# Score accumulators of one bank instead of two, and result stores behind the next unit's scores, in a fused encoder layer

## The chip, the cores and the metric

The kernel runs on one core of one Trainium2 chip. The metric is the device time of one execution in microseconds (us), the median of several runs. Before the change it is 2105.86 us (three runs, 2105.69 to 2107.47).

Engines are named as in the profile: PE (matmuls; PEld is its weight load), DVE (vector engine), ACT (scalar engine), POOL (GpSimd), SP (issues DMAs). ACT issues DMAs too; those rows have the name ACTq. PSUM is the memory that PE writes its sums to. It has eight banks; one bank holds 512 float32 numbers in each of 128 partitions.

## The reference

One layer of a bidirectional encoder over two sequences, one of 1024 tokens (prompt) and one of 512 (sample), 1024 features. Tokens lie on a grid 64 wide.

```python
xn = rmsnorm(x);  z = xn @ w_in     # -> qa, ka, va, qb, kb, vb, ga, gb
o_a = gqa_attention(rope(rmsnorm(qa)), rope(rmsnorm(ka)), va)      # branch A
# branch B: 8 heads of 64; each query sees a window of 8 x 16 tokens of the grid
s = einsum('bqhd,bkhd->bhqk', qi, kb) * scale + bias
s = where(mask, s, -1e30);  p = softmax(s);  o_b = einsum('bhqk,bkhd->bqhd', p, vb)
merged = sigmoid(ga) * (o_a @ w_proj_a) + sigmoid(gb) * (o_b @ w_proj_b)
x = x + merged @ w_out
x = x + square(relu(rmsnorm(x) @ w_mlp_up)) @ w_mlp_down
y = rmsnorm(x)
```

## The kernel before

The sample sequence is worked on first, then the prompt, each through the input projection, branch A, branch B, the gated merge and the output projection; the MLP of both follows. Float32 matmuls are made of three: each operand is split into a high and a low part (names ending in h and l), and L266, L267 and L268 multiply high by high, low by high and high by low parts. The splits are an ACT copy (L255) and a DVE subtraction (L261).

**Branch B** (phase phB, around 170 to 310 us for the sample and 765 to 1040 for the prompt) is cut into units. A unit is one head and one strip of 16 columns of the prompt's grid, 32 units in all, or one head and a pair of strips of the sample's, 16 units. A unit has two halves: two halves of the rows for the prompt, the two strips for the sample. In names such as sbs1_7_2 stand the sequence (0 sample, 1 prompt), the head and the strip; a last 0 or 1 is the half (for the sample, the strip).

*s_unit* makes the scores. For each half POOL adds bias and mask (bms, L1150), PE runs two matmuls (sbs, L1164) of 384 key columns (256 for the sample), DVE adds the bias, negates and keeps the minimum (sbss, and the read of its accumulator, msbs, both L1166), and ACT takes the Exp (pbs, L1170). Both halves of a unit write into one PSUM tile of two banks, each into its own bank.

*planes* (prompt only) scales and splits the probabilities (L1184 and L1185 on DVE, hbs on ACT L1191 and DVE L1192), and SP issues their DMA transposes into bhs (L1195). *t_unit* does the same job for the sample with PE transposes (L1209 to L1215).

*v_unit* multiplies by the values (obs, L1237), brings the sum out on ACT (ot_Bs, L1244) and DVE (os_Bs, L1245; L1250 for the sample), and lets POOL add its two parts (L1263). For heads 0 to 5, ACT then issues the store of os_Bs to DRAM (obds, L1265, 64 KB, 36 stores in all). For heads 6 and 7 the result stays on the chip: ACT copies it (oXs, L1275) and DVE subtracts (L1276). Two os_Bs tiles take turns.

The loop over units is a pipeline of three: in its turn i it calls planes(i-1), s_unit(i), t_unit(i-1) and v_unit(i-2). In between it pulls matmuls of other work into the gaps, so that PE has something to do while DVE, ACT and POOL are busy with a unit: the projections of the gates (gps), of the next heads' queries and keys (pqbs, pkbs), and near the end of the loop branch A's output projection (ppas), whose sums DVE multiplies by gates (mAs, L1047).

What the program says is not the order on the engines. A scheduler sorts the instructions of each engine by priority and by when it thinks that they can run; each engine then executes its list in order, and waits at an instruction until all that it depends on is done. Dependencies go by whole tiles: an instruction that writes to a tile of which another engine has yet to read a part waits for that read, whatever columns each of them touches.

**PSUM** is shared by two pools: pbig, two tiles of two banks, from which a unit's scores are taken, and pmm, four tiles of one bank for everything else in this phase.

Of the kernel before, what the change touches and what calls it, by code (L numbers as in the profile page):

```python
# [19 lines left out]
P = 128  # L20
D = 1024
NC8 = D // P
HD = 64
# [51 lines left out]
def encoder(ctx: ExitStack, tc: tile.TileContext, xs, outs, w):  # L75
# [11 lines left out]
    rawp = mix.enter_context(tc.tile_pool(name="rawp", bufs=3))  # L87
    sgp = mix.enter_context(tc.tile_pool(name="sgp", bufs=2))
    s8l = mix.enter_context(tc.tile_pool(name="s8l", bufs=NLEFT))
    pbig = mix.enter_context(tc.tile_pool(name="pbig", bufs=2, space=bass.MemoryType.PSUM))  # L90
    pmm = mix.enter_context(tc.tile_pool(name="pmm", bufs=4, space=bass.MemoryType.PSUM))


    hd = dram.tile([NTOK, D], F32, name="hd")
# [2 lines left out]
    def phase(name, bufs=2):  # L97
        return tc.tile_pool(name=name, bufs=bufs, reuse_waits="tile")
# [8 lines left out]
        return pmm.tile([P, 512], F32, tag="mm", name=name)  # L107

    def big(name):
        return pbig.tile([P, 1024], F32, tag="big", name=name)  # L110


    ident = cst.tile([P, P], F32, name="ident")
# [379 lines left out]
    def run(tr, nxt, first):  # L493
# [560 lines left out]
        nkc = kr_n // 4  # L1054
        nkey = kr_n * 32
        nq = rows * 16
        with phase(f"phB{N}") as ph:
            JN = 3 - halves
            msk = ph.tile([P, halves * 3, nkey], BF16, tag="msk", name=f"msk{N}", bufs=1)
# [71 lines left out]
            qk = {}  # L1131
            W = halves * P

            def s_unit(u):
                h, js = u
                s = big(f"sb{N}_{h}_{js[0]}")
                p = ph.tile([P, 2, nkey], F32, tag="pb", name=f"pb{N}_{h}_{js[0]}", bufs=2)
                nm_, l, rl = (
                    sml.tile([P, 8], F32, tag=n_, name=f"{n_}b{N}_{h}_{js[0]}") for n_ in ("ms", "ss", "rs")
                )  # L1140
                for x, (j, hf) in enumerate((j, hf) for j in js for hf in range(halves)):
                    nm = f"{N}_{h}_{j}_{hf}"
                    ct = (0, 1, 1, 2)[j]
                    c0 = (0, 8, 24, 32)[j]
                    jr = (16, 8, 8, 0)[j]
                    r0 = 0 if hf == 0 else 4
                    ir = 4 if hf == 0 else 0
                    if j != 2:
                        bm = ph.tile([P, nkey], F32, tag="bm", name=f"bm{nm}", bufs=4)
                        nc.gpsimd.tensor_tensor(  # L1150
                            bm.rearrange("p (r c) -> p r c", c=32),
                            rects[h][:, ir : ir + kr_n, jr : jr + 32],
                            msk[:, hf * 3 + ct, :].rearrange("p (r c) -> p r c", c=32),
                            op=ALU.add,
                        )
                        bms[hf] = bm
                    bm = bms[hf]
                    q0 = j * (T // 4) + hf * P
                    so = s[:, x * 512 : x * 512 + nkey]
                    for i in range(2):  # L1160
                        kv = qk[h // 2][1][h % 2][:, i, :].rearrange("p (r c) -> p r c", c=GRID_W)[
                            :, r0 : r0 + kr_n, c0 : c0 + 32
                        ]
                        nc.tensor.matmul(so, qk[h // 2][0][:, h % 2, q0 : q0 + P], kv, start=(i == 0), stop=(i == 1))  # L1164
                    sb = ph.tile([P, nkey], F32, tag="sb", name=f"sbs{nm}", bufs=2)
                    nc.vector.tensor_tensor_reduce(  # L1166
                        out=sb, in0=so, in1=bm, op0=ALU.add, op1=ALU.min, scale=-1.0, scalar=3e38,
                        accum_out=nm_[:, x : x + 1],
                    )
                    nc.scalar.activation(  # L1170
                        p[:, x], sb, AF.Exp, bias=nm_[:, x : x + 1], scale=-1.0, accum_out=l[:, x : x + 1]
                    )
                    if JN == 2:
                        nc.vector.reciprocal(rl[:, x : x + 1], l[:, x : x + 1])
                        nc.gpsimd.tensor_scalar(p[:, x], p[:, x], rl[:, x : x + 1], 1.0, op0=ALU.mult, op1=ALU.mult)
                PT[u] = p
                if JN == 1:
                    rls[u] = l, rl
# [39 lines left out]
            def v_unit(u):  # L1218
                h, js = u
                nm = f"{N}_{h}_{js[0]}"  # L1220
                hl = PT.pop(u)
                o = mm(f"ob{nm}")
                if halves == 2:
                    ov = o.rearrange("p (i h q) -> p i h q", i=2, h=2)
                    seq = [
                        (ov[:, :, a:b, :], kc, js[0], hl[:, kc, :, a:b, :], n == 0, n == 3)
                        for n, (kc, a, b) in enumerate([(1, 0, 2), (2, 0, 2), (0, 0, 1), (3, 1, 2)])
                    ]
                else:
                    ov = o.rearrange("p (x i q) -> p x i q", x=2, i=2)  # L1230
                    seq = [
                        (ov[:, x], kc, j, hl[:, 2 * x + kc, :, 0, :], kc == 0, kc == 1)
                        for x, j in enumerate(js)
                        for kc in range(2)
                    ]
                for dst, kc, j, part, first_, last_ in seq:
                    nc.tensor.matmul(  # L1237
                        dst, strips[h][:, j, kc, :], part, start=first_, stop=last_, skip_group_check=True
                    )
                ps = slice(64 * (h % 2), 64 * (h % 2) + 64) if h >= 6 else slice(0, 64)  # L1240
                t = ph.tile([HD, 512], F32, tag="ot", name=f"ot_B{nm}", bufs=1)
                b = ph.tile([P, 512], F32, tag="os", name=f"os_B{nm}", bufs=2)[ps]
                if JN == 1:
                    nc.scalar.activation(t, o[HD:P], AF.Copy, scale=svs[HD:P, 6 + h // 4 : 7 + h // 4])  # L1244
                    nc.vector.scalar_tensor_tensor(  # L1245
                        b, o[0:HD], svs[0:HD, 6 + h // 4 : 7 + h // 4], t, op0=ALU.mult, op1=ALU.add
                    )
                else:
                    nc.scalar.activation(t, o[HD:P], AF.Copy)
                    nc.vector.tensor_tensor(b, o[0:HD], t, op=ALU.add)  # L1250
                if halves == 2:
                    b0, b1 = b[:, 0:256], b[:, 256:512]
                    def place(t_):
                        return t_[:, js[0] * 256 : js[0] * 256 + 256]

                else:
                    bv = b.rearrange("p (x i q) -> p x i q", x=2, i=2)
                    b0, b1 = bv[:, :, 0, :], bv[:, :, 1, :]
                    def place(t_):
                        v = t_.rearrange("p (j q) -> p j q", q=P)  # L1260
                        return v[:, 1:3] if js[0] == 1 else v[:, 0:4:3]

                nc.gpsimd.tensor_tensor(b0, b0, b1, op=ALU.add)  # L1263
                if h < 6:
                    nc.scalar.dma_start(place(obd[h * HD : h * HD + HD, :]), b0)  # L1265
                    return
                if not oX3:
                    oX3.append(slot([P, 2, T], F32R, f"oX{N}_1_3"))
                def token(t_):
                    v = t_.rearrange("p (r j c) -> p j r c", j=4, c=16)  # L1270
                    return v[:, js[0]] if halves == 2 else v[:, 1:3] if js[0] == 1 else v[:, 0:4:3]

                hi, lo = (token(oX3[0][ps, i, :]) for i in range(2))
                b0 = b0.rearrange("p (r c) -> p r c" if halves == 2 else "p x (r c) -> p x r c", c=16)
                nc.scalar.activation(hi, b0, AF.Copy)  # L1275
                nc.vector.tensor_tensor(lo, b0, hi.bitcast(F32), op=ALU.subtract)  # L1276

            prep(0)
            fill.add(gate(3328, zg[1]))
# [11 lines left out]
            for i in range(n + LS + LV):  # L1291
# [5 lines left out]
                    planes(units[i - 1])  # L1297
                if i < n:
                    s_unit(units[i])
                    if units[i][1][0] == 1 and units[i][0] + 1 < 8:  # L1300
                        prep(units[i][0] + 1)
                    if i % per == (6 if JN == 1 else 2) and i + 2 < n:
                        while held:
                            held.pop(0)()
                        qp = qkproj(i // per + 1, wqk, qk)
                        for _ in range(NC8):
                            next(qp)
                    if i % per == per - 1 and qp is not None:
                        for _ in qp:
                            pass  # L1310
                        qp = None
# [15 lines left out]
                        next(qp)  # L1327
                fill.pull(f - f // 2)
                if 0 <= i - LS - LV < n:
                    v_unit(units[i - LS - LV])  # L1330
            fill.drain()


        mgs = {}
        with phase(f"phG{N}") as ph:
            oX = load_o(1) + oX3
# [792 lines left out]
```

## Time and profile before

| | before |
|---|---|
| median of the runs | 2105.86 us (2105.69 to 2107.47) |
| the profiled execution | 2107.32 us |
| its span, from first to last instruction | 2105.5 us |
| PE busy | 2071.3 us, 98% of the span |
| DVE busy | 1500.9 us, 71% |
| ACT busy | 1137.8 us, 54% |
| POOL busy | 330.4 us, 16% |
| mean granted PE clock | 0.997 |

The profile is of one execution. In a row of a timeline stand the start, the time taken, the engine, the line, the operation, out<-in with tile names without their numbers, shapes, and, in square brackets, how long the engine had been idle before it and what ended that. Matmuls overlap, so the rate of PE is read from the starts of successive ones and not from the time that one takes. In a list of waits stand the waiting instruction, what it waited for, the sum in us, how often, and the longest.

### The profile page before, as it was taken

To read this page: it belongs to the slowest core of one execution; us is meant where nothing else is said; L and a number is where in the kernel's file an instruction comes from. 1 tells how busy PE (TensorE), PEld (TensorE's weight loads), DVE (VectorE), ACT (ScalarE), POOL (GpSimd) and SP (SyncE) were. 2 spreads that over 40 slices of the span, in tenths; PEclk is the share of its full clock that TensorE was granted. 3 is DMA by queue.
4 is the path that set the end of the run, shared out by engine and by line. 5 is a ranking of instruction groups with operands and counts; after the bars stand their busy time and mean duration, and the time that the engine had idled before them with its cause. 6 is when DMAs were issued, how large, how long until landed. Compare 5 with 4: busy or idle time off the path is not lost.

```text
span 2105.5 us, 31206 instructions
## 1 busy us (share of the span) xinstructions
PE 2071.3 (98%) x10521; PEld 1783.3 (85%) x10521; DVE 1500.9 (71%) x2885; ACT 1137.8 (54%) x2351; POOL 330.4 (16%) x445
## 2 busy tenths in 40 slices
PE   9999999999999999999999999999999999999998
PEld 8888878987797777777788999999999988888887
DVE  6775786778668855667864877787777777669563
ACT  5654654657647755666522666565556634334442
POOL 3232420422232222322101100012000000000000
PEclk9999999999999999999999999999999999999999
DMA  6546557645525565666764566478444899688561
GB/s 188 154 126 181 150 181 246 190 104 101 125 58 131 113 139 126 149 148 157 210 204 140 185 200 197 157 244 222 143 157 153 286 348 342 213 279 277 159 204 66
DMA packets 442569, 376.59 MB, mean 179 GB/s; under 512 B 167456, under 2 KB 380072, under 8 KB 442409
## 3 DMA queue, kind: packets, MB, share of 16 engines
q1 hardware_dynamic: 400471, 306.67, 50.4%
q10 hardware_dynamic: 36258, 50.88, 7.1%
q0 software_dynamic: 5680, 17.04, 2.9%
q8 instruction: 83, 1.36, 0.3%
q14 instruction: 77, 0.63, 0.1%
HBM read 263.29 MB, written 85.79 MB: 166 GB/s over the span
## 4 chain that ended last, share of the span: by engine, by line
PE 52%; DVE 1%; issue 1%; DMA 1%; ACT 1%; SPq 0%; POOL 0%; ACTq 0%; POOLq 0%; DVEq 0%
PE dn L267 7%; PE dn L268 7%; PE dn L266 7%; PE uc L266 2%; PE ud L266 2%; PE uc L268 2%; PE ud L268 2%; PE ud L267 2%; PE uc L267 2%; PE ua L266 2%; PE ua L268 2%; PE ua L267 2%; PE ops L267 1%; PE ops L268 1%; PE ops L266 1%; PE ub L266 1%
## 5 line engine op out<-in xcount | busy, mean ns | idle before, releaser
L268 PE MATMUL dn<-wd,al 128*128 128x512 f32 (+1 forms) x624 | 242.7, 389 | 0.0
L267 PE MATMUL dn<-wd,ah 128*128 128x512 f32 (+1 forms) x624 | 242.7, 389 | 0.0
L266 PE MATMUL dn<-wd,ah 128*128 128x512 f32 (+1 forms) x624 | 242.6, 389 | 0.0
L1542 ACT ACTIVATE ah<-ar 128x512 fp32r<-128x512 f32 x168 | 104.4, 627 | 202.5 <-PE dn L267 184.7
L1543 DVE TENSOR_TENSOR al<-ar,ah 128x512 fp32r<-128x512 f32 x168 | 115.0, 692 | 76.1 <-ACT ah L1542 68.1
L266 PEld LDWEIGHTS dn<-wd,ah 128*128 128x128 f32 x624 | 117.2, 188 | 24.2
L268 PEld LDWEIGHTS dn<-wd,al 128*128 128x128 f32 x624 | 117.2, 188 | 24.0
L267 PEld LDWEIGHTS dn<-wd,ah 128*128 128x128 f32 x624 | 117.2, 188 | 24.0
L903 ACT ACTIVATE ps<-ss,nms 128x1024 f32<-128x1024 f32 (+1 forms) x96 | 93.2, 971 | 33.9 <-DVE ls L911 11.9
L900 DVE TENSOR_REDUCE nms<-ss 128x1 f32<-128x1024 f32 (+1 forms) x96 | 99.7, 1039 | 13.9 <-PE ss L898 13.1
L266 PE MATMUL gpss<-xs_0h,w_gs 128*128 128x512 f32 x256 | 102.7, 401 | 1.4 <-DVE ptls L938 1.3
L267 PE MATMUL gpss<-xs_0l,w_gs 128*128 128x512 f32 x256 | 101.0, 395 | 0.0
L268 PE MATMUL gpss<-xs_0h,w_gs 128*128 128x512 f32 x256 | 100.7, 393 | 0.0
L251 POOL TENSOR_TENSOR rs_f<-ms_f,mhalf 128x1 f32<-128x1 f32 x6 | 4.0, 668 | 590.7 <-DVE ms_f L247 590.7
L1542 ACT ACTIVATE A<-S 128x512 fp32r<-128x512 f32 x128 | 76.1, 624 | 30.7 <-DVE S L1605 26.2
L1150 POOL TENSOR_TENSOR bms<-rects,msks 128x384 f32<-128x384 f32 (+1 forms) x72 | 64.2, 896 | 154.6 <-DVE msbs L1166 114.5
L1661 ACT ACTIVATE c<-c 128x384 f32<-128x384 f32 x97 | 50.7, 524 | 67.7 <-DVE c L1660 67.7
L1543 DVE TENSOR_TENSOR A<-S,A 128x512 fp32r<-128x512 f32 x128 | 84.5, 686 | 3.8 <-ACT A L1542 3.8
L1170 ACT ACTIVATE pbs<-sbss,msbs 128x384 f32<-128x384 f32 (+1 forms) x96 | 55.3, 577 | 58.8 <-POOL os_Bs L1263 23.3
L266 PE MATMUL uc<-B,A 128*128 128x384 f32 x256 | 85.7, 335 | 0.0
L266 PE MATMUL ud<-B,A 128*128 128x384 f32 x256 | 85.7, 335 | 0.0
L268 PE MATMUL uc<-B,A 128*128 128x384 f32 x256 | 85.7, 335 | 0.0
(391 smaller groups left out, 6369.2 us busy)
## 6 DMA issues: line engine op xcount, KB each, us to landing
ar<-ud SPq DMA_DIRECT2D x120, 512.0 KB
br<-in_w_mlp_down_dram SPq DMA_DIRECT2D x72, 512.0 KB
rawu<-in_w_mlp_up_dram SPq DMA_DIRECT2D x64, 512.0 KB
ud<-c ACTq DMA_DIRECT2D x128, 192.0 KB
raw_gs<-in_w_in_dram SPq DMA_DIRECT2D x32, 512.0 KB
zgs<-sgs ACTq DMA_DIRECT2D x48, 256.0 KB
ud<-cs SPq DMA_DIRECT2D x64, 192.0 KB
vss<-vds SPq DMA_DIRECT2D x256, 32.0 KB
```

Source lines behind the costliest of these rows:

```text
L251: nc.gpsimd.tensor_tensor(r[:, :n], m[:, :n], mhalf[:, :n], op=ALU.pow)
L266: nc.tensor.matmul(out, ah, bh, start=start, stop=False, **kw)
L267: nc.tensor.matmul(out, ah, bl, start=False, stop=False, **kw)
L268: nc.tensor.matmul(out, al, bh, start=False, stop=stop, **kw)
L900: nc.vector.tensor_reduce(nm_, s, axis=AX.X, op=ALU.max, negate=True)
L903: nc.scalar.activation(p, s, AF.Exp, bias=nm_, accum_out=l)
L1150: nc.gpsimd.tensor_tensor(bm.rearrange("p (r c) -> p r c", c=32), rects[h][:, ir : ir + kr_n, jr : jr + 32], msk[:, hf * 3 + ct, :].rearra ...
L1170: nc.scalar.activation(p[:, x], sb, AF.Exp, bias=nm_[:, x : x + 1], scale=-1.0, accum_out=l[:, x : x + 1])
L1542: nc.scalar.activation(hi, src, AF.Copy)
L1543: nc.vector.tensor_tensor(lo, src, hi.bitcast(F32), op=ALU.subtract)
L1661: nc.scalar.activation(t, t, AF.Relu)
```

## The change

1. In phase phB the score tiles come from a pool of four tiles of one bank, instead of two tiles of two banks. Each half of a unit takes its own tile. The pool is opened ahead of the phase and the one of two-bank tiles is opened again behind it. The pool pmm is now allocated ahead of it.
2. What follows POOL's addition in v_unit (the store for heads 0 to 5, the copy and the subtraction for heads 6 and 7) is put on a list and issued behind the s_unit of the loop's next turn, or, past the last s_unit, ahead of the next v_unit and at the end.

```diff
-    pbig = mix.enter_context(tc.tile_pool(name="pbig", bufs=2, space=bass.MemoryType.PSUM))
     pmm = mix.enter_context(tc.tile_pool(name="pmm", bufs=4, space=bass.MemoryType.PSUM))
+    bigs = mix.enter_context(ExitStack())
+    pbig = {}
+
+    def set_bigs(n):
+        bigs.close()
+        pbig.clear()
+        pbig[n] = bigs.enter_context(tc.tile_pool(name=f"pbig{n}", bufs=4 // n, space=bass.MemoryType.PSUM))
+
+    set_bigs(2)
...
-        return pbig.tile([P, 1024], F32, tag="big", name=name)
+        return pbig[2].tile([P, 1024], F32, tag="big", name=name)
...
+        set_bigs(1)
         with phase(f"phB{N}") as ph:
...
+            late = []
+
+            def put():
+                while late:
+                    late.pop(0)()
+
             def s_unit(u):
                 h, js = u
-                s = big(f"sb{N}_{h}_{js[0]}")
...
-                    so = s[:, x * 512 : x * 512 + nkey]
+                    so = pbig[1].tile([P, 512], F32, tag="one", name=f"sb{nm}")[:, 0:nkey]
...
                 nc.gpsimd.tensor_tensor(b0, b0, b1, op=ALU.add)
                 if h < 6:
-                    nc.scalar.dma_start(place(obd[h * HD : h * HD + HD, :]), b0)
+                    late.append(lambda: nc.scalar.dma_start(place(obd[h * HD : h * HD + HD, :]), b0))
                     return
...
-                nc.scalar.activation(hi, b0, AF.Copy)
-                nc.vector.tensor_tensor(lo, b0, hi.bitcast(F32), op=ALU.subtract)
+
+                def cut():
+                    nc.scalar.activation(hi, b0, AF.Copy)
+                    nc.vector.tensor_tensor(lo, b0, hi.bitcast(F32), op=ALU.subtract)
+
+                late.append(cut)
...
                     s_unit(units[i])
+                    put()
...
                 if 0 <= i - LS - LV < n:
+                    if i >= n:
+                        put()
                     v_unit(units[i - LS - LV])
+            put()
             fill.drain()
 
 
+        set_bigs(2)
```

In the changed file lines of this phase stand further down: L1164 becomes L1178, L1166 L1180, L1170 L1184, L1237 L1251, L1265 L1279, and L266 L274.

The scheduler's order moves with it in phase phB only. On PE, at the scores of unit 1_1_1, before:

```order
L1237 MATMUL obs1_0_2_9154<-bhs1_0_2_9039,vss1_0_8746 128x2x128
L1164 MATMUL sbs1_1_1_9176<-kBs1_0_1_8783,qBs1_0_8781 128x384 x2
L266 MATMUL gpss1_3328_1_0_9091<-xs1_0h1_4287,w_gs1_3328_1_8960 128x512
L267 MATMUL gpss1_3328_1_0_9091<-xs1_0l1_4289,w_gs1_3328_1_8960 128x512
...
L1164 MATMUL sbs1_1_1_9176<-kBs1_0_1_8783,qBs1_0_8781 128x384 x2
```

and with the change:

```order
L1251 MATMUL obs1_0_2_9186<-bhs1_0_2_9069,vss1_0_8774 128x2x128
L1178 MATMUL sbs1_1_1_0_9213<-kBs1_0_1_8811,qBs1_0_8809 128x384 x2
L1178 MATMUL sbs1_1_1_1_9221<-kBs1_0_1_8811,qBs1_0_8809 128x384 x2
L274 MATMUL gpss1_3328_1_0_9122<-xs1_0h1_4311,w_gs1_3328_1_8989 128x512
L275 MATMUL gpss1_3328_1_0_9122<-xs1_0l1_4313,w_gs1_3328_1_8989 128x512
```

The second half's pair stood four gate matmuls behind the first half's and now follows it directly. So it is with 47 of the 48 units; the one other is 1_7_2, of which the first half has moved into the next place.

On PE, where the scores of heads 6 and 7 begin, before:

```order
L268 MATMUL ppas1_0_1_11044<-oXs1_0_3_10913,w_pas1_0_10889 128x512
L1164 MATMUL sbs1_6_0_11100<-kBs1_3_0_10699,qBs1_3_10698 128x384 x2
L1164 MATMUL sbs1_6_3_11178<-kBs1_3_0_10699,qBs1_3_10698 128x384 x2
L1164 MATMUL sbs1_6_0_11100<-kBs1_3_0_10699,qBs1_3_10698 128x384 x2
L1164 MATMUL sbs1_7_1_11255<-kBs1_3_1_10700,qBs1_3_10698 128x384 x2
L1164 MATMUL sbs1_6_3_11178<-kBs1_3_0_10699,qBs1_3_10698 128x384 x2
L266 MATMUL ppas1_1_0_11066<-oXs1_0_0_10895,w_pas1_1_10985 128x512
```

and with the change:

```order
L276 MATMUL ppas1_0_1_11098<-oXs1_0_3_10965,w_pas1_0_10941 128x512
L1178 MATMUL sbs1_6_0_0_11159<-kBs1_3_0_10750,qBs1_3_10749 128x384 x2
L1178 MATMUL sbs1_6_0_1_11167<-kBs1_3_0_10750,qBs1_3_10749 128x384 x2
L1178 MATMUL sbs1_6_3_0_11237<-kBs1_3_0_10750,qBs1_3_10749 128x384 x2
L1178 MATMUL sbs1_6_3_1_11245<-kBs1_3_0_10750,qBs1_3_10749 128x384 x2
L1178 MATMUL sbs1_7_1_0_11315<-kBs1_3_1_10751,qBs1_3_10749 128x384 x2
L1178 MATMUL sbs1_7_1_1_11323<-kBs1_3_1_10751,qBs1_3_10749 128x384 x2
L1178 MATMUL sbs1_7_2_0_11382<-kBs1_3_1_10751,qBs1_3_10749 128x384 x2
L274 MATMUL ppas1_1_0_11120<-oXs1_0_0_10947,w_pas1_1_11038 128x512
```

Five pairs in a row have become seven; the second half of 7_1 and the first half of 7_2 have come forward. The second half of 7_2 stays about a hundred instructions behind, where both halves of it stood before.

On ACT, at the store of unit 1_0_3, before:

```order
L1244 ACTIVATE ot_Bs1_0_3_9303<-obs1_0_3_9298,svs_95 64x512
L1170 ACTIVATE pbs1_1_0_9321,ssbs1_1_0_9323<-sbss1_1_0_0_9329,msbs1_1_0_9322 128x384
L1265 DMA obds1_4442<-os_Bs1_0_3_9304 64x256
L1170 ACTIVATE pbs1_1_0_9321,ssbs1_1_0_9323<-sbss1_1_0_1_9336,msbs1_1_0_9322 128x384
L1191 ACTIVATE hbs1_1_2_1_9316<-pbs1_1_2_9259,rsbs1_1_2_9262 128x3x128
```

and with the change:

```order
L1258 ACTIVATE ot_Bs1_0_3_9337<-obs1_0_3_9332,svs_95 64x512
L1184 ACTIVATE pbs1_1_0_9353,ssbs1_1_0_9355<-sbss1_1_0_0_9362,msbs1_1_0_9354 128x384
L1184 ACTIVATE pbs1_1_0_9353,ssbs1_1_0_9355<-sbss1_1_0_1_9370,msbs1_1_0_9354 128x384
L1205 ACTIVATE hbs1_1_2_1_9349<-pbs1_1_2_9290,rsbs1_1_2_9293 128x3x128
L1279 DMA obds1_4466<-os_Bs1_0_3_9338 64x256
```

The store has moved from between the two Exps of the next scores to behind them and one more instruction. About a third of the stores move like this one; the others keep their places among the Exps.

## The prediction

> **What bounds the kernel now.** I read the page first, then PE's waits by stretch, then the busy windows of those stretches, then single moments on the timelines. The page says which engine sets the time.
>
> ```profile
> span 2105.5 us, 31206 instructions
> PE 2071.3 (98%) x10521; PEld 1783.3 (85%) x10521; DVE 1500.9 (71%) x2885; ACT 1137.8 (54%) x2351; POOL 330.4 (16%) x445
> ```
>
> PE is idle for 2105.5 - 2071.3 = 34.2 us in all. A change of this kind can win that idle time where it lies in branch B, whatever PE loses there to a lower clock, and what a matmul takes too long to start; nothing else. So the question is what PE waits for in branch B: about 170 to 310 us for the sample sequence, 765 to 1040 for the prompt. The waits of PE, for the three stretches 170 to 310, 765 to 960 and 960 to 1040, in this order:
>
> ```profile
> PE sbs L1164 <- DVE msbs L1166: 0.8, 3, 0.4
> PE ppas L266 <- ACT sgs L528: 0.7, 1, 0.7
> PE sbs L1164 <- DVE msbs L1166: 6.1, 11, 1.5
> PE sbs L1164 <- DVE msbs L1166: 6.6, 4, 3.8
> ```
>
> Columns are us in total, times, longest. One wait owns nearly all of it, 13.5 us in 18 pieces: a score matmul waits until DVE has read an accumulator. It is nearly always the second half of a unit, and what it waits for is the read of the first half, because both halves are one tile of two banks. The windows of the same stretches (length, busy time of PE, PEld, DVE, ACT, POOL, granted clock, DMA):
>
> ```profile
> 170.00:310.00 140.00, 138.00 (x680) 111.79 (x679) 94.81 (x247) 79.62 (x163) 49.96 (x72) 1.00 0.55 167
> 765.00:960.00 195.00, 188.57 (x848) 145.24 (x847) 126.03 (x314) 117.88 (x230) 52.90 (x57) 1.00 0.59 137
> 960.00:1040.00 80.00, 73.37 (x320) 55.64 (x319) 65.59 (x145) 45.01 (x90) 16.71 (x19) 0.96 0.77 185
> ```
>
> The first two have DVE at 68% and 65%, so DVE has room to follow an earlier PE. In the third it is at 82%, and the clock is not full.
>
> **The change part by part.** The order shows what moves: the second half's pair of matmuls, which stood two to six fill matmuls behind the first, now stands right behind it, on its own bank, and waits only for the read of four tiles back.
>
> *Scattered waits.* 0.8 + 6.1, and of the third stretch what its three long ones (1.52, 0.86 and 3.77, below) leave of 6.6, some 0.45: 7.3 us. With four banks PE may be two units ahead of DVE before it is held. I take 7.0; the bounds are 7.3, and 3 if half of them come back at the next instruction that needs DVE.
>
> *The longest wait.* PE, then DVE around it:
>
> ```profile
> 999.93 0.60 PE L1164 MATMUL sbs<-kBs,qBs 128*128 128x384 f32 x2
> 1001.08 0.40 PE L266 MATMUL ppas<-oXs,w_pas 128*128 128x512 f32 x1
> 1005.25 0.73 PE L1164 MATMUL sbs<-kBs,qBs 128*128 128x384 f32 x2 [3.77 <-DVE msbs L1166]
> 1005.77 0.63 PE L267 MATMUL ppas<-oXs,w_pas 128*128 128x512 f32 x1
> 1008.75 0.53 PE L268 MATMUL ppas<-oXs,w_pas 128*128 128x512 f32 x1
> 1009.12 0.39 PE L266 MATMUL ppas<-oXs,w_pas 128*128 128x512 f32 x1
> ```
>
> ```profile
> 998.09 0.76 DVE L261 TENSOR_TENSOR w_pbs<-raw_pbs,w_pbs 128x256 fp32r<-128x256 f32 x2 [2.30 <-ACT w_pbs L255]
> 1004.63 0.55 DVE L1166 CUSTOM_DVE_ANT_0 sbss<-sbs,bms 128x384 f32<-128x384 f32 x1
> 1005.11 0.08 DVE L1166 DVE_READ_ACCUMULATOR2_ANT msbs<- 128x1 f32 x1
> ```
>
> DVE had lost 2.30 us to a weight that was still in flight and then worked through its queue up to the scores of 7_2, while PE had work ready behind. After the change the second half of 7_2 waits for the bank of 6_3's second half, read long before. So 3.8 us go; 1.9 is the bound below, if half of DVE's lateness meets PE at its next use.
>
> *The clump.* Near 974 us five pairs of score matmuls stand in a row before, seven after, on four banks, so the fifth to seventh still wait:
>
> ```profile
> 974.33 0.87 PE L1164 MATMUL sbs<-kBs,qBs 128*128 128x384 f32 x4
> 976.72 0.62 PE L1164 MATMUL sbs<-kBs,qBs 128*128 128x384 f32 x2 [1.52 <-DVE msbs L1166]
> 978.21 1.52 PE L1164 MATMUL sbs<-kBs,qBs 128*128 128x384 f32 x4 [0.86 <-DVE msbs L1166]
> ```
>
> ```profile
> 971.42 0.56 DVE L1166 CUSTOM_DVE_ANT_0 sbss<-sbs,bms 128x384 f32<-128x384 f32 x1 [1.00 <-PE sbs L1164]
> 974.00 2.19 DVE L1192 SCALAR_TENSOR_TENSOR hbs<-pbs,rsbs,hbs 128x384 f16<-128x384 f32 x2
> 976.12 0.54 DVE L1166 CUSTOM_DVE_ANT_0 sbss<-sbs,bms 128x384 f32<-128x384 f32 x1
> 976.59 0.08 DVE L1166 DVE_READ_ACCUMULATOR2_ANT msbs<- 128x1 f32 x1
> ```
>
> The seventh pair needs three score reads and one hbs done on DVE: 3 x 0.55 + 0.1 + 2.19 / 2 = 2.9 us from the start of the first read. That start was 1.8 us behind the clump's (974.33 to 976.12); DVE's idle 1.00 at 971.42 goes and PE comes some 0.45 earlier, so I put it at 1.2. The seventh pair then starts 4.1 us after the clump's start. Unhindered it would start after six pairs: four matmuls took 0.87 to the end of the last, which with 0.34 for that last one is 0.177 from start to start, so 2.1 us. A wait of 2.0 stays of 2.38: gain 0.4, bounds -0.6 (DVE comes as late as before, 1.8) and 2.4.
>
> *The clock.* Both long stops are followed by slow matmuls. The windows of 10 us show it (the clock is the third number from the end):
>
> ```profile
> 970.00:980.00 10.00, 7.62 (x34) 5.68 (x32) 7.92 (x22) 6.78 (x16) 6.04 (x7) 0.92 0.47 106
> 980.00:990.00 10.00, 10.00 (x44) 7.36 (x43) 9.42 (x22) 5.24 (x11) 2.27 (x3) 0.91 1.07 237
> 1000.00:1010.00 10.00, 6.23 (x22) 4.89 (x21) 8.46 (x19) 5.98 (x13) 3.21 (x4) 0.83 0.57 157
> ```
>
> Behind the wait of 3.77, eight matmuls took from 1005.77 to 1009.12, 3.35 us; at the 0.23 apart of 1009.12 onwards they take 1.84. One drop costs 1.5. I take the second away and leave the clump's: 1.5, bounds 0 and 3.0. [...]
>
> *Opening a pair.* Where no wait shows, a pair still starts slowly:
>
> ```profile
> 818.11 0.60 PE L1164 MATMUL sbs<-kBs,qBs 128*128 128x384 f32 x2
> 818.55 0.40 PE L266 MATMUL pqbs<-xs_1h,w_bqs 128*128 128x512 f32 x1
> 819.48 0.62 PE L1164 MATMUL sbs<-kBs,qBs 128*128 128x384 f32 x2
> 819.94 0.40 PE L267 MATMUL pqbs<-xs_1l,w_bqs 128*128 128x512 f32 x1
> ```
>
> The pair holds PE for 0.44 (818.11 to 818.55), the second half's for 0.46, against 2 x 0.177 = 0.354 in the clump's first row: about 0.09 for each pair that stands alone. 47 of the 48 second halves now follow their first half directly: 47 x 0.09 = 4.2. I take 3.5; bounds 0 (the cost belongs to the bank, not to standing alone) and 4.6.
>
> *Stores and cuts.* The deferral hardly changes ACT's order: in about a third of the 36 stores it moves the store from between a unit's two Exps to behind them. What it touches:
>
> ```profile
> ACT pbs L1170 <- POOL os_Bs L1263: 23.3, 16, 2.7
> L1265 ACTq DMA_DIRECT2D obds<-os_Bs x36: 452/453/641, 204.8 to 986.9; - x36
> L1275 ACT ACTIVATE oXs<-os_Bs x12: 400/416/420, 295.1 to 1036.0; 64x256 fp32r<-64x256 f32 x12
> DVE os_Bs L1245: 0.4, 1
> ```
>
> The first row is ACT held at a store until POOL has added, and so the second Exp too; the last is DVE held once by a store in flight (from the list of who waited for the store). Behind the store on ACT stand the next Exp and hbs, and for these DVE waits. ACT is busy 118 of 195 us and PE waits for none of it, so I cost the step at nothing: the cover is the two units between a unit's scores and its v_unit. On POOL a few bias adds change places with their neighbours; on SP the transposes of hbs and some 32 KB loads of vss pass each other by a row or two, and the two queues gain no transfer. Without the cover, each of the prompt's eight deferred cuts brings the last projection 0.42 us later: bounds -3.4 and, for Exps that no longer stand behind a store, +1.
>
> *What comes back.* In the last stretch DVE would have to do its 65.6 us in about 80 - 6.6 = 73, 90%. I give back 1.2; bounds 5 and 0.
>
> Sum: 7.0 + 3.8 + 0.4 + 1.5 + 3.5 - 1.2 = 15.0. The profiled execution took 2107.3, so 2092.3; it lies 1.5 above the median of 2105.9, so in terms of that median 2090.8, say **2091**.
>
> **The rivals.**
>
> *Everything comes off.* DVE keeps up, the clump is smooth and the clock full: 7.3 + 3.8 + 2.4 + 3.0 + 4.6 = 21.1, which is 2084.7. For it: DVE idles in the clump for PE (1.00 at 971.42). Against: seven pairs on four banks.
>
> *The wait moves to DVE's next customer.* If DVE sets the pace of 960 to 1040, the 6.6 us return as waits of evacuated accumulators or of transposed planes, the clock drops stay, and half of the rest is kept: (0.8 + 6.1 + 4.2) / 2 = 5.5, so 2100.4. For it: the third window's 82%. Against: DVE lost 2.30 there to a transfer, not to work.
>
> [...]
>
> *It does not do what it says.* If these waits were for DVE's rate and not for the shared tile, the same time is lost elsewhere: about 2105.
>
> *Slower: the stores hold DVE.* There are two os_Bs buffers. A store that is issued later frees its buffer later, and DVE's L1245, which stands ahead of the next score reads, waits for it, as it did for 0.4 us. It decides from where the 24 stores of the prompt each hold DVE, and PE behind it, for (15.0 + 4.2) / 24 = 0.8 us; at 0.85 each the kernel is at 2105.9 - 15.0 + 20.4 = 2111. Against: a store moves by one Exp at most, and only in a third of the cases.
>
> **How the numbers follow.** The forecast has 0.47, everything 0.20, DVE's next customer 0.19, the clock 0.03, nothing 0.07, slower 0.04. A measurement here can tell about 0.2%, 4.2 us, from no change. So faster 0.89, the same 0.07, slower 0.04. The range goes from 2084, which takes in the full gain, to 2102, which takes in the moved wait.
>
> **What would show it.** Right: PE's wait for msbs falls from 13.5 to about 2, all of it near 974; no wait near 1005 and a granted clock of 1.00 there; second halves of 0.36 instead of 0.46 from start to start; the stretch from 765 to 1040 shorter by about 13. Wrong: new rows of PE waiting for mAs, os_Bs, bhs or sgs in the last stretch; more slow matmuls; DVE waiting for obds; or a clump that keeps both its waits and the later 3.8.

## The result and the profile after

The changed kernel takes 2089.48 us (median of four runs, 2087.87 to 2092.17) beside 2106.34 for the one before: a ratio of 0.9921, with a 95% interval of 0.9903 to 0.9938. The forecast was 2091, 2084 to 2102. The page of the profiled execution (2090.06 us):

```profile
span 2088.3 us, 31204 instructions
PE 2062.2 (99%) x10521; PEld 1782.6 (85%) x10521; DVE 1495.9 (72%) x2885; ACT 1137.3 (54%) x2351; POOL 330.1 (16%) x445
```

PE is busy 9.1 us less and idle 26.1 us instead of 34.2. The work is the same; it is busy for less time because pairs open without delay, one stretch of half clock is gone (1000 to 1010 at a granted clock of 0.83 before and 1.00 now), and a matmul overlaps with its successor where it used to run out ahead of a stop (ahead of the stop of 3.77 us one held PE from 1001.08 to 1001.48, 0.40 us, where 0.23 lie between the starts of others). PE's waits in the sample's branch B (170 to 310 us), and in the prompt's (765 to 953, and 953 to 1030):

```profile
PE ptbs L1223 <- POOL pbs L1189: 0.6, 2, 0.4
PE ppas L274 <- ACT w_pas L263: 0.6, 1, 0.6
PE ppas L274 <- ACT sgs L536: 0.3, 1, 0.3
...
PE obs L1251 <- DMA bhs<-hbs: 1.8, 2, 1.3
PE sbs L1178 <- DVE kBs L1136: 0.4, 1, 0.4
PE obs L1251 <- DVE hbs L1206: 0.3, 1, 0.3
...
PE sbs L1178 <- DVE msbs L1180: 2.1, 2, 1.7
PE obs L1251 <- DVE os_Bs L1259: 0.7, 1, 0.7
PE ppas L274 <- ACT w_pas L263: 0.3, 1, 0.3
```

The waits for msbs fell from 13.5 us to 2.1, and those 2.1 are the clump. New ones have come, of other kinds: PE now waits where the scores' work is used (obs, for the transposed planes and for os_Bs), and here and there for a weight. The windows (length, busy PE, PEld, DVE, ACT, POOL, granted clock, DMA):

```profile
170.00:310.00 140.00, 138.25 (x690) 114.21 (x689) 95.11 (x252) 80.53 (x164) 49.23 (x72) 1.00 0.56 169
765.00:950.00 185.00, 182.97 (x845) 146.48 (x845) 126.94 (x314) 118.38 (x233) 54.42 (x57) 1.00 0.62 142
950.00:1027.00 77.00, 73.16 (x323) 54.90 (x322) 62.68 (x143) 44.08 (x88) 15.94 (x19) 0.98 0.81 198
960.00:970.00 10.00, 7.74 (x28) 5.15 (x28) 8.57 (x25) 6.09 (x16) 4.30 (x6) 0.83 0.71 168
1000.00:1010.00 10.00, 9.67 (x43) 6.92 (x41) 7.91 (x18) 6.34 (x11) 0.74 (x1) 1.00 0.84 196
```

Between 100 and 2050 us of this profile only 960 to 970 is below full clock (0.83); behind the place of the former 3.77 us wait it is 1.00. The clump on PE:

```profile
959.82 1.58 PE L1178 MATMUL sbs<-kBs,qBs 128*128 128x384 f32 x8
963.13 0.62 PE L1178 MATMUL sbs<-kBs,qBs 128*128 128x384 f32 x2 [1.73 <-DVE msbs L1180]
964.14 1.12 PE L1178 MATMUL sbs<-kBs,qBs 128*128 128x384 f32 x4 [0.39 <-DVE msbs L1180]
```

Four pairs go through at once, the fifth waits 1.73 and the sixth 0.39: four banks, seven pairs, as the order said.

From the first starts of sbs, ppas and ppbs, by stage (the change was profiled three times, here and in the two repeats below):

| stage | before | after | repeats |
|---|---|---|---|
| sample: first sbs to first ppbs | 126.2 | 123.7 | 124.1, 124.1 |
| prompt: first sbs to first ppas | 196.3 | 187.6 | 188.8, 186.7 |
| prompt: first ppas to first ppbs | 67.1 | 62.1 | 61.9, 62.4 |

Together the three stages are 16.2 us shorter, and 14.8 and 16.4 in the repeats. Each other part of the program is the same within about 1 us, of either sign.

### The profile page after: what moved, and what is told of

It reads as the page before. It is cut to its first block, busy times and chain, and to the rows that moved or that the text cites. A ratio compares the mean times of both kernels' runs of the same rounds, so it can differ in the third digit from the quotient of the medians.

```text
span 2088.3 us, 31204 instructions
## 1 busy us (share of the span) xinstructions
PE 2062.2 (99%) x10521; PEld 1782.6 (85%) x10521; DVE 1495.9 (72%) x2885; ACT 1137.3 (54%) x2351; POOL 330.1 (16%) x445
## 4 chain that ended last, share of the span: by engine, by line
PE 50%; DVE 1%; DMA 0%; issue 0%; ACT 0%; POOL 0%; POOLq 0%; ACTq 0%; DVEq 0%
PE dn L275 7%; PE dn L274 7%; PE dn L276 7%; PE uc L274 2%; PE ud L274 2%; PE ud L275 2%; PE uc L275 2%; PE ud L276 2%; PE uc L276 2%; PE ua L274 2%; PE ua L275 2%; PE ua L276 2%; PE ops L276 1%; PE ops L274 1%; PE ops L275 1%; PE ub L274 1%
## 5 line engine op out<-in xcount | busy, mean ns | idle before, releaser
L274 PE MATMUL dn<-wd,ah 128*128 128x512 f32 (+1 forms) x624 | 242.3, 388 | 0.0
L274 PEld LDWEIGHTS dn<-wd,ah 128*128 128x128 f32 x624 | 117.1, 188 | 24.3
L274 PE MATMUL gpss<-xs_0h,w_gs 128*128 128x512 f32 x256 | 102.5, 400 | 1.4 <-DVE ptls L946 1.3
L1164 POOL TENSOR_TENSOR bms<-rects,msks 128x384 f32<-128x384 f32 (+1 forms) x72 | 65.4, 919 | 152.0 <-DVE msbs L1180 98.4
L274 PE MATMUL uc<-B,A 128*128 128x384 f32 x256 | 85.6, 334 | 0.0
L274 PE MATMUL ud<-B,A 128*128 128x384 f32 x256 | 85.6, 334 | 0.0
L276 PE MATMUL ud<-B,A 128*128 128x384 f32 x256 | 85.5, 334 | 0.0
L275 PE MATMUL ud<-B,A 128*128 128x384 f32 x256 | 85.5, 334 | 0.0
```

Source lines behind the costliest of these rows:

```text
L274: nc.tensor.matmul(out, ah, bh, start=start, stop=False, **kw)
L275: nc.tensor.matmul(out, ah, bl, start=False, stop=False, **kw)
L276: nc.tensor.matmul(out, al, bh, start=False, stop=stop, **kw)
L1164: nc.gpsimd.tensor_tensor(bm.rearrange("p (r c) -> p r c", c=32), rects[h][:, ir : ir + kr_n, jr : jr + 32], msk[:, hf * 3 + ct, :].rearra ...
```

## The experiments

**The whole change again**, the yardstick for what stands beside it.

> The whole change once more, as the yardstick for the three beside it. Every theory: 16 to 18 us below the kernel before, a ratio of 0.992.

2090.37 us, 0.9927 of the kernel before (0.9914 to 0.9939). And once more:

> The whole change a third time, beside the next run. Every theory: ratio 0.992 to 0.993.

2090.69 us, 0.9927 (0.9915 to 0.9940).

**Each half of the change alone.** First the deferral, with the scores of a unit in one two-bank tile as before:

```diff
-        set_bigs(1)
...
+                s = big(f"sb{N}_{h}_{js[0]}")
...
-                    so = pbig[1].tile([P, 512], F32, tag="one", name=f"sb{nm}")[:, 0:nkey]
+                    so = s[:, x * 512 : x * 512 + nkey]
...
-        set_bigs(2)
```

> Only the deferral of stores and cuts; the scores of a unit again share one tile of two banks. Theory: within 2 us of the kernel before, 2104 to 2108, with PE waiting for msbs for 12 to 15 us. Rival (the deferral has its own gain): 4 us or more below the kernel before.

2107.07 us, 1.0001 (0.9992 to 1.0010). PE's waits in the prompt, 765 to 953 and 953 to 1035:

```profile
PE sbs L1178 <- DVE msbs L1180: 6.2, 11, 1.5
PE sbs L1178 <- DVE msbs L1180: 6.9, 4, 3.4
```

They are those of the kernel before. Alone the deferral is worth nothing. Then the one-bank tiles alone:

```diff
-                    late.append(lambda: nc.scalar.dma_start(place(obd[h * HD : h * HD + HD, :]), b0))
+                    nc.scalar.dma_start(place(obd[h * HD : h * HD + HD, :]), b0)
...
-                late.append(cut)
+                cut()
```

> Only the one-bank score tiles; stores and cuts stand where they stood. The order on PE is that of the whole change, row for row. Theory (the shared tile made PE wait, the deferral does nothing): the same as the whole change within 2 us, about 2089, with PE waiting for msbs about 2 us. Rival (the deferral frees ACT, and part of the gain is its): at least 4 us slower than the whole change, 2093 or more, with ACT's waits for POOL's os_Bs ahead of an Exp back at 20 us and more where the whole change has them gone.

2092.24 us, 0.9939 (0.9927 to 0.9952), beside 2090.37 for the whole. The prompt's stages are as short as with the whole change (189.2 and 62.0 us), but the sample's is 126.9: there nothing was won. ACT's waits for POOL ahead of an Exp, which the rival expected back at 20 us, are 13.6 here, 12.3 with the whole change and 22.0 with the deferral alone: they fell with the tiles, not with the deferral. In the sample PE stands at a wait for qBs that neither the kernel before nor the whole change has there, as the repeat shows too:

> The one-bank tiles without the deferral, a second time, to settle whether the 1.9 us that lay between it and the whole change are real. Theory (the deferral does nothing): within 1.5 us of the whole change beside it, on either side. Rival (deferred stores keep ACT free in the sample's stretch, where the first run without them lost 2.8 us): 1.5 to 3 us slower again, and again most of it between 181 and 308 us, with PE waiting there for qBs.

2091.99 us, 0.9935 (0.9921 to 0.9948), beside 2090.69; the sample's stage takes 125.9. The two differences of 1.9 and 1.3 us lie within the intervals, so the times alone do not settle it; the place is the same both times. The length of the sample's stage tells more: 126.9 and 125.9 in these two, 122.9 to 124.1 in all eight profiles of kernels with one-bank tiles and the deferral (the three above and five below). From the repeat: PE's wait in the sample (170 to 310), what SP's queue waited for (240 to 275), and SP's and ACT's timelines:

```profile
PE obs L1251 <- DVE qBs L1118: 0.7, 1, 0.7
```

```profile
SPq L1081 <- DMA obds<-os_Bs: 8.3, 2, 5.8
...
249.96 13.35 SPq L1081 DMA_DIRECT2D vss<-vds  x16
263.41 4.54 SPq L1020 DMA_DIRECT2D rawos<-oads  x4
```

```profile
266.14 0.63 ACT L263 ACTIVATE oXs<-rawos 128x512 fp32r<-128x512 f32 x1 [3.09 <-DMA rawos<-oads]
```

SP issues sixteen loads of values (vss) and behind them the reload of branch A's output (rawos). In this run one vss load stands 5.8 us until a store of os_Bs has landed; rawos comes late, ACT idles 3.09 at the copy of rawos, and the copies of the next head's queries and keys stand behind it in ACT's list, for which DVE and then PE wait. In the first run of these tiles alone it was 10.5 us in all, 6.2 the longest. The second repeat of the whole change at the same place:

```profile
SPq L1081 <- DMA obds<-os_Bs: 5.2, 3, 3.0
...
251.47 11.36 SPq L1081 DMA_DIRECT2D vss<-vds  x16
262.93 4.58 SPq L1020 DMA_DIRECT2D rawos<-oads  x4
```

**One store alone.** In that stretch ACT's order differs by few stores. So the one-bank tiles, with only the store of unit 0_3_0 deferred:

```diff
-                    late.append(lambda: nc.scalar.dma_start(place(obd[h * HD : h * HD + HD, :]), b0))
+                    st = lambda: nc.scalar.dma_start(place(obd[h * HD : h * HD + HD, :]), b0)
+                    late.append(st) if (N, h, js[0]) == ("s0", 3, 0) else st()
...
-                late.append(cut)
+                cut()
```

> The one-bank tiles, and of the 48 deferred steps only one: the store of unit 0_3_0 in the sample, which moves from between two Exps to behind the second. Theory (that store holds up SP: in both runs with the one-bank tiles alone the sixteen vss loads of SP's queue waited 6 us for a store to land, the loads of rawos came 2 to 3 us later, ACT and then PE stood for them): the sixteen vss loads take about 11 us instead of 13.4 to 14.3, PE does not wait for qBs, the sample's stretch from the first sbs to the first ppbs is 124 us instead of 126 to 127, and the time is that of the whole change, about 2090. Rival (the deferral as a whole shifts the stores, or the difference is chance): the stretch stays at 126 and the time at 2092.

2089.49 us, 0.9926 (0.9913 to 0.9940), and the sample's stage 123.7 us, as with the whole change. SP again:

```profile
SPq L1081 <- DMA obds<-os_Bs: 4.1, 2, 3.3
...
250.50 11.20 SPq L1081 DMA_DIRECT2D vss<-vds  x16
261.81 4.69 SPq L1020 DMA_DIRECT2D rawos<-oads  x4
```

Of the 48 deferred steps this one does what the deferral does, and it does it to SP, not to ACT or PE. The loads of vss read vds and not what the stores write (obds), and yet one of them stands until a store of os_Bs has landed: for 5.8 us at the longest with no store deferred, 3.3 with this one, and 3.0 in the second repeat of the whole change. The kernel before has such waits at the same place, 8.3 us in three pieces, 3.7 the longest. Why a load waits for a store, and why the store's place changes how long, the waits do not show; nor is it shown that this is all of the 2 us.

**Two tiles of one bank** in place of four:

```diff
-        pbig[n] = bigs.enter_context(tc.tile_pool(name=f"pbig{n}", bufs=4 // n, space=bass.MemoryType.PSUM))
+        pbig[n] = bigs.enter_context(tc.tile_pool(name=f"pbig{n}", bufs=2, space=bass.MemoryType.PSUM))
```

> The whole change with two score tiles of one bank in place of four: each half still has its own tile, but only two are in flight, so a half waits for the read of the same half one unit earlier. Theory (the tile that both halves share made PE wait, not the number of banks): the scattered waits stay away, PE waits for msbs outside the clump near 965 for under 1 us, and the time is within 3 us of the whole change, the clump alone being worse. Rival (PE needs to be two units ahead of DVE): 5 us or more of msbs waits outside the clump, 2096 or more.

2092.46 us, 0.9936 (0.9924 to 0.9949). PE's waits for msbs in 765 to 953 and 953 to 1030:

```profile
PE sbs L1178 <- DVE msbs L1180: 0.9, 2, 0.5
PE sbs L1178 <- DVE msbs L1180: 2.4, 2, 2.0
```

Of 6.1 us in eleven waits 0.9 in two are left, with half the banks. It was the tile that the two halves shared, not the number of banks. The time is some 2 us above that of the whole change, within the intervals; the trace has more to wait for at obs, 2.3 us for the last transposes, followed by a lower clock (0.96 and 0.87 in the windows from 1010 to 1030).

**Fill matmuls between the halves**, to price the opening of a pair:

```diff
+                    if x == 0:
+                        fill.pull(1)
...
-                fill.pull(f // 2)
+                fill.pull(max(f // 2 - (i < n), 0))
```

> The whole change, but one group of three fill matmuls is asked for between the two halves of a unit and one fewer behind them, so that the second half's pair stands three fill matmuls behind the first in 39 of 48 units, as it stood in the kernel before, on its own bank. Theory (a pair that stands alone costs 0.09 more to open): 39 x 0.09 = 3.5 us slower than the whole change, about 2093, with no wait for msbs beyond those of the whole change. Rival (the opening cost came from the wait for the read that had only just ended, not from standing alone): within 1 us of the whole change, and second halves of 0.36 us from start to next start.

2093.46 us, 0.9935 (0.9922 to 0.9947); the time would fit the theory, the trace does not. A unit in this run, and one of the whole change:

```profile
797.23 0.60 PE L1178 MATMUL sbs<-kBs,qBs 128*128 128x384 f32 x2
797.67 0.40 PE L274 MATMUL gpss<-xs_0h,w_gs 128*128 128x512 f32 x1
...
798.36 0.51 PE L1178 MATMUL sbs<-kBs,qBs 128*128 128x384 f32 x2
798.72 0.39 PE L274 MATMUL pqbs<-xs_0h,w_bqs 128*128 128x512 f32 x1
```

```profile
796.42 0.96 PE L1178 MATMUL sbs<-kBs,qBs 128*128 128x384 f32 x4
797.22 0.39 PE L274 MATMUL pqbs<-xs_0h,w_bqs 128*128 128x512 f32 x1
```

The second half holds PE for 0.36 us (798.36 to 798.72) though it stands alone, against 0.46 before; the first, behind obs, for 0.44 as ever. In the whole change both take 0.80 = 0.44 + 0.36. The trace of before says when: the 25 second halves of the prompt that held PE 0.45 to 0.47 us began 0.05 to 0.06 us after DVE's read of the first half had ended, with idle time in front of them or without; the three that held it 0.36 (at 778.07, 837.07 and 1013.16) began 0.16 us or more after it. So the 0.10 belonged to the wait on the shared tile, which cost it even where no idle time shows. What this run loses, if it does (its interval overlaps that of the whole change), lies elsewhere: obs waits 2.2 for os_Bs and 2.3 for the last transposes after 1000 us.

**The clump, taken out of both kernels.** Branch A's output projection of the prompt begins a turn earlier. In the old kernel:

```diff
-                if i == n - (6 if first else 9):
+                if i == n - (6 if first else 10):
```

> The kernel before, with the projection begun one turn earlier and nothing else: two-bank tiles, stores in place, no clump. Theory (the waits on the shared tile and the clump are two costs): the two waits of 2.4 us near 974 and their clock drop of 1.5 go, the scattered ones of 7 us stay, so 2102 to 2104. Rival (the clump was only where a common lateness of DVE showed): within 1 us of the kernel before, with new msbs waits of 2 us and more between 980 and 1040.

2103.11 us, 0.9984 (0.9975 to 0.9992). In the old kernel this is a gain of 3 us. The waits left in the prompt (765 to 953, 953 to 1030):

```profile
PE sbs L1164 <- DVE msbs L1166: 5.8, 11, 1.5
PE sbs L1164 <- DVE msbs L1166: 5.6, 5, 3.4
```

The same edit in the changed kernel:

> The whole change, with branch A's output projection of the prompt begun one loop turn earlier, so that its operands are there when the fill matmuls before it run out. In the order on PE the seven pairs in a row near 965 are gone; each unit's two pairs stand about 30 rows apart. Theory (the clump costs its waits and the clock behind them): the msbs wait of 2.1 us and the half clock of some 1.5 us go, so about 3.6 us below the whole change, near 2086, and a granted clock of 1.00 in all windows of the stretch. Rival (DVE sets the pace there): the same 2 to 4 us come back as waits for os_Bs, bhs or mAs, and the time is within 1 us of the whole change.

2092.07 us, 0.9933 (0.9919 to 0.9946): no gain. The clump's waits and its half clock are gone (1.00 in every window of 10 us from 950 to 1040), and in their place stand (same two stretches):

```profile
PE obs L1251 <- DMA bhs<-hbs: 2.2, 2, 1.7
PE obs L1251 <- DVE msbs L1180: 1.9, 1, 1.9
...
PE obs L1251 <- DVE os_Bs L1259: 2.0, 2, 1.6
PE obs L1251 <- DMA bhs<-hbs: 1.8, 1, 1.8
```

From the first sbs to the first ppbs the prompt takes 250.4 us with the edit and 249.7 without (250.7 and 249.1 in the repeats). PE now meets the far end of a unit's chain: what it is let off earlier it waits for at obs in this run. With more fill in the first turns, where the transposes of the first units are late:

```diff
-                    f = 0 if i == n - 10 else 5 + (i % 3 > 0) if i < n - 8 else 7
+                    f = 0 if i == n - 10 else 8 if 0 < i < 4 else 5 + (i % 3 > 0) if i < n - 8 else 7
```

> As the run with the earlier projection, and with two or three more fill groups in each of the loop turns 1 to 3 of the prompt, where PE now waits 1.8 to 2.3 us for the transposes of the first units. Theory: another 1.5 to 2 us, about 2084.5, and no obs wait for bhs before 800 us. Rival (the fill taken here is missing later): the wait moves behind 940, and the time is that of the run with the earlier projection or above it.

2093.33 us, 0.9934 (0.9922 to 0.9947). The waits before 800 us are gone and one of 2.03 stands at 927: they moved, as the rival said, though not as far as it said. Last, two banks for obs alone, taken from the scores:

```diff
-                o = mm(f"ob{nm}")
+                o = pbig[1].tile([P, 512], F32, tag="ob", name=f"ob{nm}", bufs=2)
...
-                    so = pbig[1].tile([P, 512], F32, tag="one", name=f"sb{nm}")[:, 0:nkey]
+                    so = pbig[1].tile([P, 512], F32, tag="one", name=f"sb{nm}", bufs=2)[:, 0:nkey]
```

> The run with the earlier projection, with the four banks of the pool divided: two for scores and two for obs, which then no longer share banks with the fill matmuls. Theory (after the change PE stops where an obs cannot get a bank): the two waits of obs for os_Bs, 2.0 us between 990 and 1005, go, and the time is about 2090. Rival (DVE is late there as a whole): they come back as waits for msbs, bhs or mAs of the same length, within 1 us of the run with the earlier projection.

2095.0 us, 0.9952 (0.9939 to 0.9964), some 3 us above the run it is built on, though the intervals overlap. The waits for os_Bs are gone; in the last stretch (953 to 1030) stand

```profile
PE obs L1251 <- DMA bhs<-hbs: 2.3, 1, 2.3
PE sbs L1178 <- DVE msbs L1180: 1.2, 3, 0.5
PE ppas L276 <- DVE w_pas L269: 1.0, 1, 1.0
```

and before it 1.7 for a vss load and 1.5 for qBs. None of these kernels is faster than the whole change beyond the intervals.

## Why the prediction was right

The time of 2091 stands against 2089.5, 2090.4 and 2090.7. By its own steps:

- *The scattered waits and the longest one*, 7.0 and 3.8: right. All 11.1 us of msbs waits outside the clump are gone, and the run with two tiles shows that the shared tile was their cause.
- *The clump*: right in mechanism and size. A wait of 2.0 was forecast to stay; it is 2.1 (1.73 at the fifth pair and 0.39 at the sixth).
- *The clock*: right for the drop behind the 3.77 us wait, which is gone. That behind the clump stays in the first profile (0.83 in one window of 10 us, which is 1.7 us lost) and in the first repeat (mean granted clock of the execution 0.998 in both), but not in the second repeat (0.999), whose clump waits just as long, 2.1 us (the last section has an estimate of the reason).
- *Opening a pair*, 3.5: the size was near, the reason wrong. The prediction laid the cost on a pair that stands alone; the run with fill between the halves shows a pair that stands alone at 0.36. It went with the wait on the shared tile. In the trace of before it was paid 25 times in the prompt and 13 times in the sample (0.33 to 0.35 there instead of 0.24), three of these behind a visible wait: 38 times 0.10 is 3.8.
- *Stores and cuts at nothing*: right for the deferral alone (1.0001), wrong beside the one-bank tiles, where the stores left in their places cost some 2 us in the sample and moving one of them takes that away. That is a loss avoided and not a gain over the kernel before, whose PE does not wait for qBs there. The step looked at ACT and DVE; of SP it said only that the queues gain no transfer. That SP's loads wait for stores stood in the trace of before (16.1 us in five pieces), and the step makes nothing of it.
- *What comes back*, 1.2: too small and put in the wrong place. New waits of PE sum to 4.1: 0.6 in the sample (1.5 there now, 0.9 of other kinds before), 2.5 in 765 to 953, and 1.0 behind 953; in the repeats the sum is 5 to 6. Most are at obs, 1.8 of them for the transposes of the first units, and not for DVE in the last stretch.
- *A term that the sum does not have*: a matmul ahead of a stop runs out before PE stands, as at 1001.08 (0.40 us where 0.23 lie between the starts of others). By the starts in the traces, from 178 to 308 and 764 to 952 us, the fill matmuls of gates, queries and keys just ahead of a score pair or a stop held PE 4.0 us longer in all than at the 0.23 of the others, stops not counted, and 0.8 after the change: 3.2 us won.

The last two are errors of 2.9 and 3.2 us that run opposite ways, so it is in part luck that the number came out this near. With the measured sizes the terms are 11.1 + 0.3 + 1.5 + 3.8 + 3.2 - 4.1 = 15.8, beside 16.2 for the three stages.

Of the rivals, the one in which the wait moves to DVE's next customer happened to the change in small part (4.1 us came back for the 11.4 of msbs waits that went), and to all that was tried on top of it: the clump taken out bought 3 us in the old kernel and nothing in the new one. The clock did not fall more often: between 100 and 2050 us it fell once (at 965.54) where it had fallen twice, and it was 1.00 from 765 to 950. The rival in which deferred stores hold DVE did not happen either: DVE's wait for a store in flight, 0.4 us before, is not among those after.

## What to carry to other kernels

Where a scheduler tracks dependencies by tile, two halves that are written and read at different times should be two tiles, even if the banks are the same ones: two tiles of one bank in place of two of two banks took away 85% of the prompt's scattered waits. When the named wait is gone, ask which later instruction on the same engine uses the result, since that is where the next edit's gain may be swallowed, as it was here. A DMA issue that moves by one place can change how long the loads of another queue wait (8.3 us in two pieces here, 4.1 with one store moved), so the waits of the DMA queues belong to the reading too.

## What the runs showed of the hardware that was not expected

Of two stops of PE of some 2 us, one was followed by half clock and the other was not. In the run with the earlier projection and more fill, one of 2.03 was and a longer one of 2.39 near 1015 was not. On PE's timeline:

```profile
927.38 0.81 PE L1251 MATMUL obs<-bhs,vss 128*128 128x512 f16 x4 [2.03 <-DMA bhs<-hbs]
1015.50 0.70 PE L1251 MATMUL obs<-bhs,vss 128*128 128x512 f16 x3 [2.39 <-DMA bhs<-hbs]
```

Behind the first, eight fill matmuls took 3.39 us (928.74 to 932.13) where at 0.23 apart they take 1.84: that stop cost 1.55 us more than itself. Behind the second the clock is 1.00 in both windows of 10 us from 1010 to 1030.

In the traces of the kernels before and after, each spell of half clock between 100 and 2050 us lasts 3.41 us, at a granted clock of 0.50: 978.31 to 981.73 and 1005.62 to 1009.03 before, 965.54 to 968.95 after. The two falls of the kernel before lie 27.31 us apart, eight times that length. Windows of this length in the run with more fill, one of them the spell itself (PE's busy time is the second number, the clock the third from the end):

```profile
925.34:928.75 3.41, 1.38 (x10) 1.15 (x10) 2.43 (x7) 2.44 (x6) 0.33 (x1) 1.00 0.74 102
928.75:932.16 3.41, 3.41 (x10) 2.65 (x10) 2.03 (x7) 1.86 (x6) 3.05 (x4) 0.50 0.62 123
1010.68:1014.09 3.41, 2.43 (x11) 1.68 (x9) 3.31 (x6) 1.10 (x2) 0.14 (x1) 1.00 0.65 161
1014.09:1017.50 3.41, 2.00 (x10) 1.56 (x11) 0.65 (x2) 1.10 (x2) 0.72 (x1) 1.00 0.76 218
```

The stop of 2.03 lies in one window, which is idle for 2.03 us, and the next runs at half clock. The stop of 2.39 is cut in two, 0.98 and 1.41 of idle time. Windows laid in the same way over the traces of before and after, from 100 to 2050 us, have 2.38 and 3.04 us of idle time ahead of the two falls before, and 1.54 ahead of the one after; the next most, 1.15 before and 1.33 after, are followed by a clock of 1.00. That the idle time within one such window decides, and not the length of the stop, is an estimate from these four falls; what sets the limit is not shown. The three profiles of the whole change differ at the same length of wait: the clump waits 2.1 us in each, and the mean granted clock of the execution is 0.998, 0.998 and 0.999.
